# The opening of a two-layer diffusion backbone: token loads first, weights of the conditioning held in the array, first projection products fed one feature tile at a time

## The chip, the cores and the metric

One core of a Trainium2 chip runs the kernel. The metric is device time in microseconds, the median of several runs of the program.

## The reference

The reference is a two-layer backbone over 512 latent tokens and 256 context tokens of width 1024. Each layer starts from a conditioning vector `c` (latents) or `c_ctx` (context). What matters here is the beginning of layer 0:

```
s_c, s_cc = silu(c), silu(c_ctx)
sh1, sc1, g1, sh2, sc2, g2 = split(s_c @ w_ada[0] + b_ada[0], 6)     # w_ada[0]: 1024 x 6144; the same with s_cc for the context
h  = rms_norm(x,   norm_mix[0]) * (1 + sc1)  + sh1
hc = rms_norm(ctx, norm_mix[0]) * (1 + csc1) + csh1
p, pc = h @ w_in[0], hc @ w_in[0]                                    # w_in[0]: 1024 x 6144
```

After it come three mixers (retention, grouped attention, pooling), a gated merge, an output projection and a feed-forward part (dense in layer 0, eight experts of which each token takes two in layer 1). All of it is in 32-bit floats.

## The kernel before

Features stand on the 128 partitions, so a feature dimension of 1024 is eight tiles `k` (KT = 8), and the tokens (T0 = 768: 512 latent, 256 context) lie along the free dimension. A product in full precision is made of three fast passes: a value is split into a high part and a low part, and TensorE (PE) computes high x high, low x high and high x low (lines 330 to 332, in `proj`). The class `Stream` (from line 40) holds all weights in their order of use. Its `pump` loads 1 MB pieces into `raw` tiles (two buffers) through the queue of SP, and splits halves into `wh` (ScalarE, ACT, line 94) and `wl` (VectorE, DVE, line 95). `take(n)` hands out n halves.

Each engine runs its instructions in one order. Outside the experts of layer 1 a planner of the framework writes that order: it takes the instructions by their place in the program, but lets a later one go ahead where its own cost estimates say that the earlier one is not ready. It also places all waits. Tiles come from pools with a fixed count of buffers, and a new tile waits until the old user of its buffer has finished.

The opening (lines 985 to 1113) works as follows.

- **Loads.** The queue of SP issues the six token tiles `xtok` (128 tokens each, 512 KB, line 1013) between four pieces of `w_ada` (`araw`, 1 MB, line 1017, three buffers). ACT's queue issues the small vectors (`crow`, `vrow`, `rdb`).
- **`turn(t)`** takes the squares of a token tile on ACT (line 1045), transposes its eight feature tiles on PE (line 1050) and copies them from PSUM to `xT`, half on ACT and half on DVE.
- **Conditioning.** `scol` holds silu of `c` and `c_ctx` as columns. Only column groups j = 0 to 3 of `w_ada` (512 columns each: shift and scale of the first norm) are needed here. For j = 0, 1 and 3 `ada_direct` makes the two columns of `scol` the standing operand and streams 512 columns of `w_ada` past them, eight times, summed in PSUM (line 279). The result is two rows, which ACT copies (line 281) and PE turns into columns (line 284). A 32-bit product of this kind appears in the trace as two passes, so that a group is 16 passes. For j = 2 DVE multiplies and adds (lines 158 and 160, 16 operations), GpSimd (POOL) cuts the sums into three parts, and PE adds over the partitions with 24 tiny products (line 234).
- **Norm.** `rr`, 1 / rms of each token, is spread over the partitions by PE (line 1082); DVE multiplies `xT` with it (line 1086) into `u`, which lies in the memory of `xtok`. `modulation` turns shift and scale into `AB` (lines 269 and 270). `norm0(k)` makes the high part `hh` on ACT (line 1101) and the low part `hl` on DVE (lines 1105 and 1106); for k = 3 and 7 ACT does the work of line 1105. Groups j = 0 and 2 give `AB` for k = 0 to 3, groups j = 1 and 3 for k = 4 to 7.
- **Products.** `mix_phase(0)` then runs the units of the mixers, `u0` and `u1` first, each for 512 latent and 256 context tokens.

Of the kernel before, what the change touches and what calls it, by code (L numbers as in the profile page):

```python
# [35 lines left out]
# vec-tile rows (rows of 128 values, turned into columns on the chip)  # L36
# [76 lines left out]
def tile_backbone(  # L113
# [19 lines left out]
    # ---------------------------------------------------------------- weights, in order of use  # L133
# [11 lines left out]
    def ada_sum(li, j, nv):  # L145
        """512 columns of w_ada, multiplied and summed over k ahead of the sum over partitions."""
# [28 lines left out]
    # column tiles of w_in: name -> tile index  # L175
# [7 lines left out]
    # ---------------------------------------------------------------- constants  # L183
# [14 lines left out]
    def rsqrt(out_ap, v, n, make=None):  # L198
        """out = v ** -0.5 for a small [128, n] tile, or a wide one with tiles from make."""
# [36 lines left out]
    # ---------------------------------------------------------------- plan of the layers  # L236
# [5 lines left out]
    st = {}          # state handed from one part to the next  # L242
    later = []       # steps to be placed between the groups of products that follow
# [10 lines left out]
    # ================================================================ small vectors, modulation  # L254
# [3 lines left out]
    AB = vp.tile([128, 2, 2, KT], F32, name="AB")      # stream (latent/context), A or B, k  # L258
# [5 lines left out]
    def modulation(li, which, norm_row, k0=0, k1=KT):  # L264
        """A = gain * (1 + scale), B = shift of the norm in front of a mixer, for both streams."""
# [6 lines left out]
    def ada_direct(j, raws, mid=None):  # L272
        """The same columns for layer 0, all of the sum on the tensor engine."""
        p = st["mm"].tile([128, 512], F32, name="mm")
        for k in range(KT):
            w = raws[k // 4].rearrange("p (k m) -> p k m", k=4)[:, k % 4]
            if k == 4 and mid:
                mid()
            PE.matmul(p[:2], scol.rearrange("p (s k) -> p k s", s=2)[:, k], w, start=(k == 0), stop=(k == KT - 1))
        r = st["sp"].tile([2, 512], F32, name="adarow")  # L280
        A.activation(r, p[:2], AF.Copy)
        p2 = st["mm"].tile([128, 512], F32, name="mm")
        for q in range(4):
            PE.transpose(p2[:, 2 * q:2 * q + 2], r[:, 128 * q:128 * q + 128], ident[:2, :2])
        ada_store(0, j, 2, p2[:, :8].rearrange("p (q s) -> p s q", s=2))
# [21 lines left out]
    # ================================================================ mixers  # L307
    class Mixer:
# [6 lines left out]
        def proj(self, name, both):  # L315
            """One column tile of w_in for all tokens (both) or for those that are queries."""
# [19 lines left out]
            return fn  # L336

# [60 lines left out]
        def stat(self, name, parts):  # L398
            """(mean square + eps) ** -0.5 of a head's queries or keys, [128, tiles]."""
# [24 lines left out]
        def spread(self, r, n):  # L424
            """[128, n] per token -> the same value on all partitions, [128, n * 128] in PSUM."""
# [11 lines left out]
        # ---- retention  # L437
        def retention(self):
            li, T, mt = self.li, self.T, st["mt"]
            for pr in range(2):  # L440
                yield from self.wait(f"rq{pr}", f"rk{pr}")
                # of each head: its queries' high part twice, its keys' high part and low part
# [19 lines left out]
                for h in (2 * pr, 2 * pr + 1):  # L462
# [4 lines left out]
                    # values by token, centred over the head's width: the group norm's mean  # L467
# [11 lines left out]
                    # decays as a function of query - key  # L479
# [80 lines left out]
        # ---- attention  # L560
# [88 lines left out]
        # ---- pooling  # L649
# [133 lines left out]
    def square_in(mt, c0, c1):  # L783
        """Adds the square of one feature tile of x to the running sum."""
# [63 lines left out]
    # ================================================================ dense feed-forward  # L848
# [67 lines left out]
    # ---------------------------------------------------------------- order of all the weights  # L916
# [8 lines left out]
    def plan_layer(li):  # L925
        m = mixers[li]
        for nm in order[li].split():
            if nm.startswith("ada"):
# [35 lines left out]
    def run(ph, gen=None):  # L964
        """The units of a phase; gen is advanced by a step in front of each and at its ticks."""
# [12 lines left out]
    # ================================================================ start: inputs, modulation, first norm  # L978
# [24 lines left out]
    with tc.tile_pool(name="start", bufs=1, reuse_waits="tile") as sp, tc.tile_pool(name="start_ps", bufs=8, space=PSUM, reuse_waits="tile") as mm:  # L1003
        st["mm"], st["sp"] = mm, sp
        st["accr"] = lambda t: (lambda r: [r[:, :512], r[:, 512:]])(sp.tile([128, D], F32, name="junk"))
        xtok = sp.tile([128, 6, D], F32, name="xtok")
        crow = sp.tile([16, 128], F32, name="crow")
# [7 lines left out]
        def load_ada(j, h):  # L1015
            r = rawp.tile([128, 2048], F32, name="raw") if (j, h) == (3, 0) else sp.tile([128, 2048], F32, name="araw", bufs=3)
            SY.dma_start(r.rearrange("p (k m) -> p k m", k=4), ada_src(0, j, h))
# [13 lines left out]
        # conditioning vectors as columns: silu  # L1031
        p = mm.tile([128, 512], F32, name="mm")
# [6 lines left out]
        # x with the features first, 1 / rms of each token  # L1039
        ss = sp.tile([128, 6], F32, name="ss")  # L1040
        xT = sp.tile([128, KT, T0], F32, name="xT0")

        def turn(t):
            junk = sp.tile([128, D], F32, name="junk")
            A.activation(junk, xtok[:, t], AF.Square, accum_out=ss[:, t:t + 1])
            for h in range(2):
                p = mm.tile([128, 512], F32, name="mm")
# [4 lines left out]
                if h:  # L1052
                    V.tensor_copy(dst, pv)
                else:
                    A.activation(dst, pv, AF.Copy)

        turn(0)
        p = mm.tile([128, 512], F32, name="mm")
        for li in range(2):
            PE.transpose(p[:, 128 * li:128 * li + R_N], vrow[:, li], ident[:R_N, :R_N])  # L1060
            V.tensor_copy(vec[li], p[:, 128 * li:128 * li + R_N])
            V.tensor_scalar(gnh[li], vec[li][:, R_GN:R_GN + 4], 0.5, None, op0=OP.mult)
        ada_direct(0, [raws[0, h] for h in range(2)])
        use = ada_sum(0, 2, 2)
        use(0)(raws[2, 0])
        for t in range(1, 6):
# [5 lines left out]
        acc2 = use(1)(raws[2, 1])  # L1072
        for a in ((1, 0), (1, 1), (3, 0), (3, 1)):
            load_ada(*a)
        rb = []
        u = xtok.rearrange("p a b -> p (a b)").rearrange("p (k t) -> p k t", k=KT)

        def spread_rr():
            for t0, t1 in ((0, 4), (4, 6)):
                p = mm.tile([128, 512], F32, name="mm")  # L1080
                for t in range(t0, t1):
                    PE.transpose(p[:, 128 * (t - t0):128 * (t - t0) + 128], rr[:, t:t + 1].to_broadcast([128, 128]), ident)
                rb.append(p[:, :128 * (t1 - t0)])
            for k in range(KT):
                for s, (c0, c1) in enumerate(((0, L), (L, T0))):
# [695 lines left out]
```

## Time and profile before

| | us |
|---|---|
| median of 3 runs | 3347.98 |
| lowest and highest run | 3347.87, 3348.95 |
| profiled execution, first to last instruction (span) | 3350.0 |
| PE busy in the span | 3229.9 |
| DVE busy | 2190.0 |
| ACT busy | 1449.6 |
| first product of `w_in` starts at | 55.98 |

The profiled execution is one execution of its own; its time is listed as its span alone, which is 2.0 us above the median of the runs. PE is the engine with the most work. Times in the trace count from the first instruction. The granted clock of PE has two levels, 0.5 (1.2 GHz) and 1.0 (2.4 GHz). The profile holds no record of it for the first 15.7 us and prints 1.00 there.

### The profile page before, as it was taken

Reading aid. Unit: us, or ns where it says so; the run is one execution under the profiler, and the core shown is the slowest. Engines: PE = TensorE matmul, PEld = TensorE weight load, DVE = VectorE, ACT = ScalarE, POOL = GpSimd, SP = SyncE. Lnnn points to the kernel's source line nnn. Section 1 sums busy time; section 2 is a strip of 40 time slices with the busy share of each in tenths; the row PEclk is TensorE's granted clock in tenths of the full one; section 3 lists DMA queues with packets and bytes.
Section 4 is the critical chain, followed back from the end, with each engine's and each line's share of the span. In section 5 each row is a group of like instructions: output and inputs, shape, how many; then the busy total and the mean of one; then the engine's idle time right before and its main releaser. Section 6 shows DMA issues by size and latency. Waiting matters only on the chain. (4 is left out here: it accounts for less than half of the span.)

```text
span 3350.0 us, 43794 instructions
## 1 busy us (share of the span) xinstructions
PE 3229.9 (96%) x17203; PEld 2680.2 (80%) x17204; DVE 2190.0 (65%) x3319; ACT 1449.6 (43%) x2001; POOL 277.4 (8%) x250
## 2 busy tenths in 40 slices
PE   7999999999999999999999997999999999999995
PEld 4887788888888888888778886777777777777774
DVE  6478777467454444456766566865798855885586
ACT  4334343224122111134434434754576645664564
POOL 1011221101010000000011011010000000000001
PEclk9999999999999999999999998999999999999998
DMA  7133342542232332323222447976699965996595
GB/s 267 65 109 122 107 139 92 183 151 73 79 126 98 104 113 89 101 89 124 91 85 88 132 158 255 358 252 226 229 386 359 315 244 195 321 336 238 197 326 205
DMA packets 298312, 605.00 MB, mean 181 GB/s; under 512 B 12410, under 2 KB 100636, under 8 KB 297564
## 3 DMA queue, kind: packets, MB, share of 16 engines
q1 hardware_dynamic: 285232, 555.26, 46.8%
q0 software_dynamic: 10720, 44.83, 4.1%
q8 instruction: 152, 2.49, 0.3%
q10 hardware_dynamic: 2124, 1.74, 0.2%
q14 instruction: 84, 0.69, 0.1%
HBM read 561.15 MB, written 40.63 MB: 180 GB/s over the span
## 5 line engine op out<-in xcount | busy, mean ns | idle before, releaser
L95 DVE TENSOR_TENSOR wl<-raw,wh 128x1024 fp32r<-128x1024 f32 x889 | 1052.3, 1233 | 208.9 <-ACT wh L94 195.4
L94 ACT ACTIVATE wh<-raw 128x1024 fp32r<-128x1024 f32 x892 | 884.1, 1053 | 501.5 <-PE mm L887 152.6
L331 PE MATMUL mm<-hl,wh 128*128 128x512 f32 (+1 forms) x1232 | 436.3, 354 | 6.1 <-DVE hl L846 6.1
L330 PE MATMUL mm<-hh,wh 128*128 128x512 f32 (+1 forms) x1232 | 440.5, 358 | 0.3 <-DVE mod L288 0.3
L332 PE MATMUL mm<-hh,wl 128*128 128x512 f32 (+1 forms) x1232 | 435.1, 353 | 0.0
L864 PE MATMUL mm<-hh,wh 128*128 128x512 f32 (+1 forms) x896 | 302.8, 339 | 1.0 <-ACT hh L841 1.0
L865 PE MATMUL mm<-hl,wh 128*128 128x512 f32 (+1 forms) x896 | 301.9, 337 | 1.6 <-DVE hl L846 1.0
L866 PE MATMUL mm<-hh,wl 128*128 128x512 f32 (+1 forms) x896 | 301.4, 337 | 0.0
L331 PEld LDWEIGHTS mm<-hl,wh 128*128 128x128 f32 x1232 | 235.7, 191 | 36.3 <-DVE hl L846 7.5
L330 PEld LDWEIGHTS mm<-hh,wh 128*128 128x128 f32 x1232 | 235.6, 191 | 34.6 <-issue 3.9
L332 PEld LDWEIGHTS mm<-hh,wl 128*128 128x128 f32 x1232 | 235.4, 191 | 30.3 <-issue 0.2
L865 PEld LDWEIGHTS mm<-hl,wh 128*128 128x128 f32 x896 | 170.2, 190 | 21.0 <-DVE hl L846 2.0
L1375 PE MATMUL y<-wh,gth 128*128 128x512 f32 x448 | 180.0, 402 | 6.5 <-PEq L1529 1.1
L864 PEld LDWEIGHTS mm<-hh,wh 128*128 128x128 f32 x896 | 169.9, 190 | 19.7 <-ACT hh L841 1.5
L866 PEld LDWEIGHTS mm<-hh,wl 128*128 128x128 f32 x896 | 170.1, 190 | 17.6
L1361 PE MATMUL b<-wl,xh 128*128 128x512 f32 x448 | 178.1, 398 | 4.1 <-DVE wl L95 4.1
L1359 PE MATMUL b<-wh,xh 128*128 128x512 f32 x448 | 180.9, 404 | 0.0
L1359 PE MATMUL a<-wh,xh 128*128 128x512 f32 x448 | 178.8, 399 | 1.8 <-DVEq L1529 1.0
L1376 PE MATMUL y<-wh,gtl 128*128 128x512 f32 x448 | 177.3, 396 | 0.8 <-DVE gtl L222 0.8
L160 DVE SCALAR_TENSOR_TENSOR acc<-raw,scol,acc 128x512 f32<-128x512 f32 x224 | 166.2, 768 | 18.0 <-DMA raw<-in_w_ada_dram 16.6
L1360 PE MATMUL a<-wh,xl 128*128 128x512 f32 x448 | 177.5, 396 | 0.0
L1377 PE MATMUL y<-wl,gth 128*128 128x512 f32 x448 | 177.2, 396 | 0.0
(414 smaller groups left out, 6077.5 us busy)
## 6 DMA issues: line engine op xcount, KB each, us to landing
raw<-in_moe_w_dram SPq DMA_DIRECT2D x336, 1024.0 KB, 7.6
raw<-in_w_in_dram SPq DMA_DIRECT2D x48, 1024.0 KB, 5.3
raw<-in_ffn_w_dram SPq DMA_DIRECT2D x42, 1024.0 KB, 4.9
raw<-in_w_ada_dram SPq DMA_DIRECT2D x41, 1024.0 KB, 5.3
raw<-in_w_branch_dram SPq DMA_DIRECT2D x12, 1024.0 KB, 6.2
gsp<-gst POOLq DMA_DIRECT2D x24, 384.0 KB, 2.9
gt<-gsp SPq DMA_DIRECT2D x24, 384.0 KB, 3.5
raw<-in_w_out_dram SPq DMA_DIRECT2D x8, 1024.0 KB, 5.7
```

What stands on the lines that cost most here:

```text
L94: nc.scalar.activation(hv, r, AF.Copy)
L95: (nc.gpsimd if self.n_split in self.on_pool else nc.vector).tensor_sub(lv, r, hv)
L330: PE.matmul(pv, wh[:, k], st["hh"][:, k, c0:c1], start=(k == 0), stop=False)
L331: PE.matmul(pv, wh[:, k], st["hl"][:, k, c0:c1], start=False, stop=False)
L332: PE.matmul(pv, wl[:, k], st["hh"][:, k, c0:c1], start=False, stop=(k == KT - 1))
L864: PE.matmul(pv, wh[:, k], st["hh"][:, k, c0:c1], start=(k == 0), stop=False)
L865: PE.matmul(pv, wh[:, k], st["hl"][:, k, c0:c1], start=False, stop=False)
L866: PE.matmul(pv, wl[:, k], st["hh"][:, k, c0:c1], start=False, stop=(k == KT - 1))
L1359: PE.matmul(p, xh[:, k], wh, start=(k == 0), stop=False)
L1360: PE.matmul(p, xl[:, k], wh, start=False, stop=False)
L1361: PE.matmul(p, xh[:, k], wl, start=False, stop=(k == KT - 1))
L1375: PE.matmul(y[:, n], gh[:, j], wh[:, 0, s], start=first and j == 0, stop=False)
```

## The change

The token tiles are all loaded first, then four pieces of `w_ada` (now 256 columns by all 1024 rows, four buffers), then two pieces of `w_in` with their splits. The parts of `turn` are as before; ACT copies one PSUM bank in four and DVE the rest. `ada_direct(j)` is turned round: the 128 x 128 blocks of `w_ada` stand in the array and the two columns of `scol` stream past them, so that the results are columns at once. All four groups go that way, each in two halves; each half is 2 x 8 products of two columns. Groups 0 and 2 stand before the norm, and the halves of groups 1 and 3 between its steps. After each `norm0(k)` a new function `first(k)` runs the products of that feature tile for `u0` (512 and 256 tokens) and `u1` (512 tokens), held in three PSUM banks across all eight k. `proj_open`, the first unit of the mixer phase, copies them out and computes the context tokens of `u1`. The PSUM pool of the products (three banks) is opened ahead of the opening, whose own pool shrinks from eight banks to five.

```diff
+        def ada_direct(j):
+        p = st["sps"].tile([128, 512], F32, name="sps")
+        def half(h, raw):
+            w = raw.rearrange("p (k m) -> p k m", k=KT)
+            for q in range(2):
+                for k in range(KT):
+                    PE.matmul(p[:, 4 * h + 2 * q:4 * h + 2 * q + 2], w[:, k, 128 * q:128 * q + 128],
+                              scol.rearrange("p (s k) -> p k s", s=2)[:, k], start=(k == 0), stop=(k == KT - 1))
+            if h:
+                ada_store(0, j, 2, p[:, :8].rearrange("p (q s) -> p s q", s=2))
+        return half
...
+        def proj_open(self):
+            done, (wh, wl) = st["open"]
+            for i, (c0, c1, p) in enumerate(done):
+                self.evac("u0" if i < 2 else "u1", c0, c1, p, c0 == 0, c1 == T0)
+            p = st["mm"].tile([128, 512], F32, name="mm")
...
-        for t, a in ((0, (0, 0)), (1, (0, 1)), (2, (2, 0)), (3, None), (4, None), (5, (2, 1))):
+        for t in range(6):
             load_x(t)
-            if a:
-                load_ada(*a)
+        for a in ((0, 0), (0, 1), (2, 0), (2, 1)):
+            load_ada(*a)
+        ws.raw_bufs = 1
+        ws.pump()
...
+        sum0, rb = ada_direct(0), []
+        sum0(0, raws[0, 0])
...
+        sum0(1, raws[0, 1])
+        for a in ((1, 0), (1, 1)):
             load_ada(*a)
+        sum2 = ada_direct(2)
+        sum2(0, raws[2, 0])
+        sum2(1, raws[2, 1])
+        for a in ((3, 0), (3, 1)):
+            load_ada(*a)
         modulation(0, 0, R_NMIX, 0, 4)
...
+        w0, w1 = ws.take(2)
+        open_ = [(w, c0, c1, st["mm0"].tile([128, 512], F32, name="mm")) for w, c0, c1 in ((w0, 0, L), (w0, L, T0), (w1, 0, L))]
+        def first(k):
+            for (wh, wl), c0, c1, p in open_:
+                pv = p[:, :c1 - c0]
+                PE.matmul(pv, wh[:, k], st["hh"][:, k, c0:c1], start=(k == 0), stop=False)
+                PE.matmul(pv, wh[:, k], st["hl"][:, k, c0:c1], start=False, stop=False)
+                PE.matmul(pv, wl[:, k], st["hh"][:, k, c0:c1], start=False, stop=(k == KT - 1))
+        sum1, sum3 = ada_direct(1), ada_direct(3)
+        steps = [lambda: sum1(0, raws[1, 0]), lambda: sum1(1, raws[1, 1]), lambda: sum3(0, raws[3, 0]), lambda: sum3(1, raws[3, 1])]
         for k in range(4):
             norm0(k)
-        ada_direct(3, [raws[3, h] for h in range(2)])
+            first(k)
+            steps[k]()
         modulation(0, 0, R_NMIX, 4, 8)
+        ws.raw_bufs = 2
+        ws.pump()
+        SY.dma_start(st["xsp"], xT)
+        SY.dma_start(rope_t, tab[:, :2048].rearrange("p (a b) -> p a b", a=4))
...
         for k in range(4, 8):
             norm0(k)
+            first(k)
```

## Rows read from the trace of the kernel before

**Rows 1.** The page: busy time of PE, granted clock in 40 slices.

```profile
PE 3229.9 (96%) x17203; PEld 2680.2 (80%) x17204; DVE 2190.0 (65%) x3319; ACT 1449.6 (43%) x2001; POOL 277.4 (8%) x250
...
PEclk9999999999999999999999998999999999999998
```

**Rows 2.** Windows from the first product on: busy us by engine, clock, DMA.

```profile
55.90:60.19 4.29, 4.29 (x15) 3.36 (x13) 3.41 (x9) 3.37 (x6) 0.00 (x0) 0.60 1.10 383
...
64.53:67.67 3.14, 3.14 (x18) 2.71 (x17) 1.73 (x3) 2.01 (x5) 1.47 (x2) 1.00 0.11 27
```

**Rows 3.** Groups of PE by form, 55.9 to 67.66: two of six.

```profile
L330 PE MATMUL mm<-hh,wh 128*128 128x512 f32 x10 | 4.8, 476 | 0.0
...
L330 PE MATMUL mm<-hh,wh 128*128 128x256 f32 x8 | 2.2, 281 | 0.0
```

**Rows 4.** Timeline of the opening: start us, length us.

```profile
5.54 1.97 PE L1050 MATMUL mm<-ident,xtok 128*128 128x128 f32 x8
...
8.92 1.06 ACT L1045 ACTIVATE junk<-xtok 128x1024 f32<-128x1024 f32 x1
...
37.65 1.00 DVE L217 SCALAR_TENSOR_TENSOR rr<-rs_a,rs_r 128x6 f32<-128x6 f32 x1
...
47.31 0.23 DVE L269 SCALAR_TENSOR_TENSOR AB<-mod,vec 128x4 f32<-128x4 f32 x2
...
55.98 0.50 PE L330 MATMUL mm<-hh,wh 128*128 128x512 f32 x1
```

**Rows 5.** Waits in the queue of SP, 0 to 60 us.

```profile
SPq L1013 <- DMA vrow<-in_norm_mix_dram: 5.8, 1, 5.8
```

**Rows 6.** Windows, 10 to 20 us: DMA share, GB/s last.

```profile
10.00:20.00 10.00, 9.40 (x17) 1.47 (x17) 2.07 (x12) 3.02 (x8) 0.00 (x0) 1.00 1.00 379
```

**Rows 7.** Groups by form, 0 to 64: busy us, mean ns.

```profile
L279 PE MATMUL mm<-araw,scol 128*2 128x512 f32 x40 | 22.0, 701 | 2.0 <-DVE scol L1037 2.0
...
L1106 DVE TENSOR_TENSOR hl<-xtok,hh 128x768 fp32r<-128x768 f32 x7 | 6.6, 955 | 0.1
L1101 ACT ACTIVATE hh<-xtok,AB 128x512 fp32r<-128x512 f32 x8 | 6.4, 801 | 1.2 <-DVE AB L269 1.2
...
L1105 DVE TENSOR_SCALAR xtok<-xtok,AB 128x512 f32<-128x512 f32 x6 | 3.3, 542 | 0.8 <-ACT hh L1101 0.8
```

**Rows 8.** Timeline of PE at the router of layer 1.

```profile
2006.37 1.07 PE L1182 MATMUL s<-ident,xl 128*128 128x128 f32 x8
2007.27 1.85 PE L1186 MATMUL po<-rw,xl 128*128 128x8 f32 x16
2008.98 0.46 PE L759 MATMUL mm<-hh,wh 128*128 128x256 f32 x1
2009.24 0.41 PE L760 MATMUL mm<-hl,wh 128*128 128x256 f32 x1
2009.45 0.41 PE L761 MATMUL mm<-hh,wl 128*128 128x256 f32 x1
```

**Rows 9.** Windows of the same place.

```profile
2007.27:2008.98 1.71, 1.71 (x19) 1.71 (x17) 0.36 (x2) 1.51 (x3) 0.00 (x0) 1.00 0.00 0
...
2009.10:2012.50 3.40, 3.40 (x18) 3.40 (x18) 1.41 (x6) 1.43 (x2) 0.00 (x0) 0.50 0.58 230
```

**Rows 10.** Windows of PE during the transposes of the opening.

```profile
25.95:29.36 3.41, 3.41 (x18) 0.50 1.04 386
29.36:31.20 1.84, 1.84 (x18) 1.00 1.05 388
```

**Rows 11.** Timeline of PE and its weight loads, 56 to 61.

```profile
56.86 0.33 PEld L331 LDWEIGHTS mm<-hl,wh 128*128 128x128 f32 x1
57.29 0.63 PE L331 MATMUL mm<-hl,wh 128*128 128x512 f32 x1
...
57.71 0.63 PE L332 MATMUL mm<-hh,wl 128*128 128x512 f32 x1
...
60.19 0.19 PEld L330 LDWEIGHTS mm<-hh,wh 128*128 128x128 f32 x1
```

More of the change, by code (lines that the diff above doesn't have):

```diff
@@ L270, in modulation @@
             V.tensor_copy(AB[:, s, 1, k0:k1], sh)
[L272 to L285, printed above, removed]
+    def ada_direct(j):
[9 more added lines that the diff above has]
+        return half
     def ada_store(li, j, nv, p):
@@ L336, in proj @@
             return fn
+        def proj_open(self):
+            done, (wh, wl) = st["open"]
+            for i, (c0, c1, p) in enumerate(done):
+                self.evac("u0" if i < 2 else "u1", c0, c1, p, c0 == 0, c1 == T0)
+            ready.add((0, "u0"))
+            p = st["mm"].tile([128, 512], F32, name="mm")
+            pv = p[:, :C]
+            for k in range(KT):
+                PE.matmul(pv, wh[:, k], st["hh"][:, k, L:], start=(k == 0), stop=False)
+                PE.matmul(pv, wh[:, k], st["hl"][:, k, L:], start=False, stop=False)
+                PE.matmul(pv, wl[:, k], st["hh"][:, k, L:], start=False, stop=(k == KT - 1))
+            self.evac("u1", L, T0, pv, False, True)
+            ready.add((0, "u1"))
         def evac(self, name, c0, c1, p, first, last):
@@ L927, in plan_layer @@
         for nm in order[li].split():
+            if li == 0 and nm == "u0":
+                add_cols(w_in[0], 128 * WT[nm])
+                unit("mix0", 0, lambda hs: m.proj_open())
+                continue
             if nm.startswith("ada"):
@@ L1001, in tile_backbone @@
     ws.stage(wpool, 3, limits["mix0"])
-    with tc.tile_pool(name="start", bufs=1, reuse_waits="tile") as sp, tc.tile_pool(name="start_ps", bufs=8, space=PSUM, reuse_waits="tile") as mm:
-        st["mm"], st["sp"] = mm, sp
-        st["accr"] = lambda t: (lambda r: [r[:, :512], r[:, 512:]])(sp.tile([128, D], F32, name="junk"))
+    mm0 = ExitStack()
+    st["mm0"] = mm0.enter_context(tc.tile_pool(name="mix_mm0", bufs=3, space=PSUM, reuse_waits="tile"))
+    with tc.tile_pool(name="start", bufs=1, reuse_waits="tile") as sp, tc.tile_pool(name="start_ps", bufs=5, space=PSUM, reuse_waits="tile") as sps:
+        st["sps"] = sps
         xtok = sp.tile([128, 6, D], F32, name="xtok")
-        crow = sp.tile([16, 128], F32, name="crow")
+        crow = st["adap"].tile([128, 2, 512], F32, name="acc")[:16, 0, :128]
         A.dma_start(crow[0:8], c.rearrange("o (k p) -> (o k) p", p=128))
@@ L1029, in tile_backbone @@
         A.dma_start(rdb, bass.AP(tensor=ret_decay.tensor, offset=ret_decay.offset, ap=[[0, 128], [1, 16]]))
-        p = mm.tile([128, 512], F32, name="mm")
+        p = sps.tile([128, 512], F32, name="sps")
         PE.transpose(p[:, :16], crow, ident[:16, :16])
@@ L1051, in turn @@
                 dst = xT[:, 4 * h:4 * h + 4, 128 * t:128 * t + 128]
-                if h:
+                if t % 2 and h:
+                    A.activation(dst, pv, AF.Copy)
+                else:
                     V.tensor_copy(dst, pv)
[L1054 to L1066, printed above, removed]
+        for t in range(6):
             turn(t)
@@ L1071, in tile_backbone @@
         rsqrt(rr, vv, 6)
-        acc2 = use(1)(raws[2, 1])
-        for a in ((1, 0), (1, 1), (3, 0), (3, 1)):
-            load_ada(*a)
[L1075 to L1085, printed above, removed]
-                    V.tensor_mul(u[:, k, c0:c1], xT[:, k, c0:c1], rb[s])
@@ L1088, in tile_backbone @@
-        ada_direct(1, [raws[1, h] for h in range(2)], spread_rr)
-        ada_sum_unit(0, 2, 2)([None, acc2])
-        modulation(0, 0, R_NMIX, 0, 4)
-        ws.pump()
-        SY.dma_start(st["xsp"], xT)
-        SY.dma_start(rope_t, tab[:, :2048].rearrange("p (a b) -> p a b", a=4))
-        A.dma_start(ptab, tab[:, 2048:2112].rearrange("p (a b c) -> p a b c", a=4, b=2))
-        A.dma_start(g2b, bass.AP(tensor=b_ada.tensor, offset=b_ada[1, 5 * D:6 * D].offset, ap=[[0, 128], [1, D]]))
-        A.activation(lg2, rdb, AF.Exp)
@@ L1097, in tile_backbone @@
-        V.tensor_scalar(lgc, lg2, -1.0, None, op0=OP.mult)
+        p = sps.tile([128, 512], F32, name="sps")
+        for li in range(2):
+            PE.transpose(p[:, 128 * li:128 * li + R_N], vrow[:, li], ident[:R_N, :R_N])
+            V.tensor_copy(vec[li], p[:, 128 * li:128 * li + R_N])
+            V.tensor_scalar(gnh[li], vec[li][:, R_GN:R_GN + 4], 0.5, None, op0=OP.mult)
+        sum0, rb = ada_direct(0), []
+        sum0(0, raws[0, 0])
+        for t0, t1 in ((0, 4), (4, 6)):
+            p = sps.tile([128, 512], F32, name="sps")
+            for t in range(t0, t1):
+                PE.transpose(p[:, 128 * (t - t0):128 * (t - t0) + 128], rr[:, t:t + 1].to_broadcast([128, 128]), ident)
+            rb.append(p[:, :128 * (t1 - t0)])
@@ L1637, in mix_phase @@
         T = m.T
-        with tc.tile_pool(name="mix_mm", bufs=3, space=PSUM, reuse_waits="tile") as mm, tc.tile_pool(name="mix_s2", bufs=2, space=PSUM) as s2, \
+        mm0 = st["mm0"] if li == 0 else st["mm0x"].enter_context(tc.tile_pool(name="mix_mm", bufs=3, space=PSUM, reuse_waits="tile"))
+        with tc.tile_pool(name="mix_s2", bufs=2, space=PSUM) as s2, \
                 tc.tile_pool(name="mix_po", bufs=1, space=PSUM, reuse_waits="tile") as po:
-            st["mm"], st["s2"], st["po"] = mm, s2, po
+            st["mm"], st["s2"], st["po"] = mm0, s2, po
             n3, n2 = (15, 8) if li == 0 else (8, 14)
@@ L1722, in tile_backbone @@
     ad0.close()
+    st["mm0x"] = mm1 = ExitStack()
     mix_phase(1)
+    mm1.close()
     dump("x3l", st["xl"])
```

18 lines of the change are left out of this document (14 added, 4 removed).

## Prediction

> **What bounds the kernel now.** I read the page first, then windows over the start, then the timeline of the opening, and then looked elsewhere in the trace for an operation like the one that the change brings in. PE is busy 96% of the span, and the clock was granted nearly throughout [rows 1]. The profiled execution took 3350.0 us by its span, 2.0 more than the median of the runs; I work out a difference against its trace and add it to the median. A difference of 0.2% (6.7 us) is about what a measurement of this kernel can tell from none.
>
> The opening is the exception. The first product of `w_in` starts at 55.98 us, and the clock had just fallen, so that the 11 products of 512 columns begun before 60.19 (15 PE instructions touch that window, three of them turns of a result row, one at its edge) mostly took 0.43 us each [rows 2, 4, 11]. From 60.19 to 67.66, 30 - 11 = 19 products of 512 columns and 24 of 256 fill 7.47 us, which gives 0.24 and 0.12 us at the upper level [rows 3]; PE has no gap there [rows 2]. At 0.24 the 11 first ones are worth 2.6 us, so the old kernel does as well as one whose PE runs nothing but mixer work at full speed from 60.2 - 2.6 = 57.5 us. Behind that point PE is the bound, so the change is worth what it does to this one number. I call it the equivalent start.
>
> **What is removed.** Groups 0, 1 and 3 of the conditioning cost 48 passes (40 of them 22.0 us busy, part of it at the lower level) [rows 7]. With them go the copies and turns of the result rows, and for group 2 DVE's sums, which held `rr` back to 38.65 us [rows 4]. None of this is left on the path.
>
> **Loads.** Six token tiles and one piece of `w_ada` are 4.2 MB. At the 379 GB/s of 10 to 20 us [rows 6] that is 11 us; with some 2 us before data flows, everything for the first sum has landed at about 13 us. In the old kernel the second token load stood in SP's queue 5.8 us for the landing of a small vector [rows 5]; I assume that four or five loads ahead cover such a wait, and price it under the rivals. The 48 transposes of the tokens begin at about 5.5 us, when the first tile lands [rows 4], and need 0.21 us each at the lower level (16 starts in 3.41 us, the two cut by the edges left out) [rows 10], together 10.2 us. So the first narrow pass can start between 13 us (loads) and about 19 us (if ACT's copies, behind its squares, hold the PSUM banks). I take 15. The two `w_in` loads and three splits put ahead of groups 1 and 3 are off the path: these groups wait in PE's queue far longer than for their data. The `xsp`, table and vector loads move behind the second modulation; none is read before the mixers.
>
> **The new sums.** This is the largest term. A 32-bit product appears as two passes, so a half of a group is 2 x 8 x 2 = 32 passes, each with a 128 x 128 weight load for two columns, and all four groups are 256 passes. The router holds the same form: 128 x 128 standing, eight columns streaming, 16 passes in 1.71 us, 0.107 us each at the upper level [rows 8, 9]. The load sets this pace, not the columns. At the upper level all sums are 27.4 us. The old sums of three groups were 48 passes at about 0.43, 20.6 us. So even at full clock PE has more conditioning work than before.
>
> At the lower level I find no such pass. Below, it is 0.107 (the load does not slow). Above, it is 0.213: products of 256 columns with the same size of load start 0.21 us apart there [rows 8], so a load fits into that. Weight loads grow from 0.19 to 0.33 us in the trace when the clock is halved [rows 11], so I take 0.213, and 54.6 us for all sums.
>
> Which level will it be? At the router PE did 16 passes, eight transposes and 16 passes from 2004.66 to 2008.98 without idle time, at the upper level, and at 2009.1 the clock fell to half although PE was busy throughout [rows 8, 9]. Transposes alone do not do this: after 3.4 us of them back to back the clock rose [rows 10]. So long runs of narrow passes lose the clock. I take three quarters of the narrow passes and of the products between them at the lower level; bounds are all and half.
>
> The Trainium skill (TensorE: Matmul & The Clock Gate, section "Why this matters for your kernels") advises to keep TensorE continuously busy to get and hold the full clock. By that rule the sums would run at the upper level, which is the first rival below. The router's rows disagree with it for narrow passes.
>
> **The path after the change.**
> - Groups 0 and 2, 128 passes, three quarters slow: 0.75 x 27.3 + 0.25 x 13.7 = 23.9 us. Eight transposes (spreading `rr`, turning vectors) add 1.7. `AB` is ready at 15 + 25.6 = 40.6 us, where it was 47.3 [rows 4].
> - Groups 1 and 3, 23.9 us again, and `first(0)` to `first(3)`. One is six products of 512 columns and three of 256: 1.8 us at the upper level, 3.2 at the lower. Four are 7.2 or 12.8, at three quarters 11.4. PE ends them at 75.9.
> - Then PE waits for the second modulation and `norm0(4)`: store and `AB` about 0.4, `hh` 0.8 and about 0.6, `hl` 0.96 [rows 7], 3 us with hand-overs. 78.9.
> - `first(4)` at the lower level 3.2; the next three at 1.8, by PE as well as by DVE (0.54 + 0.4 + 0.96, less where ACT takes a part) [rows 7]. 87.5.
> - All three product banks are then full. The mixer's buffers lie in the memory of the opening, so the copies out start only behind the last `norm0`. I take 1 us, between nothing and 2. 88.5.
> - Of this, eight `first` worth 14.4 us at the upper level are mixer work done. The equivalent start is 74.1 us, 16.6 later than before.
>
> In short, after `AB` the old kernel needed 10.2 us to its equivalent start. The new one must still put 13.7 to 27.3 us of sums and 4 us of waits there, and `AB` comes only some 7 us sooner. Forecast: 3348.0 + 16.6 = about 3365 us. With everything slow `AB` is at 44.0, and the start at 82.3 (+24.8, 3373), or 3377 if the first pass starts at 19. With half slow it is 65.5 (+8, 3356).
>
> **Rivals.**
> - *The upper level holds through the narrow passes.* Then `rr` limits: six squares of 1.06 us with 0.19 for the sum, three copies, and 13 small DVE operations from about 9 us [rows 4] make it ready at 20.5. With group 0's first half before it and the rest behind, `AB` is at 31.6; sums and four `first` end at 52.5, the last four with waits at 63.7; the equivalent start is 49.3, a gain of 8.2: about 3340. The tight weight-load pace speaks for it, the fall at 2009.1 [rows 9] against. Between +24.8 and -8.2 the sign turns where about three quarters of the narrow passes run at the upper level.
> - *The lower level does not slow a narrow pass.* Then groups 0 and 2 end at 32.4, groups 1 and 3 with slow products at 58.9, and the equivalent start is 57.1: no change, 3348. For it: nothing in the trace has such a pass at the lower level. Against: the loads of 0.33 us [rows 11]. The Trainium skill (same page, section "LDWEIGHTS (loading the stationary operand)") gives a load as its columns over 1.2, 107 ns, with no word of the clock's level. The pace at the upper level agrees with it, no row shows the lower, and the sum by it would be this rival's.
> - *The loads are not ahead after all.* If the wait of 5.8 us in SP's queue [rows 5] comes back ahead of the later token tiles, all moves by that: 3371.
> - *The planner's order for the rest comes out differently.* PE idles 120 us in the span, so some 10 us more or less are possible, and no row tells which. I count this at 3340, where it would hide the forecast.
>
> **Chances.** Forecast 0.64, its own range 3356 to 3377; upper level holds 0.15; slow clock without slow passes 0.11; late loads 0.05; another order 0.05. Slower: 0.64 + 0.05, and 0.01 of the third case, 0.70. Within 0.2%: 0.10 of the third and 0.03 of the second, 0.13. Faster: 0.12 + 0.05 = 0.17. The range from 3340 to 3377 holds the forecast's own range and the third case, and leaves out about half of the second, some of the fifth and the tails.
>
> **What would show it.** The windows from 15 to 80 us should show PE busy with the clock near 0.5 for most of it. Narrow passes should start 0.21 us apart there and 0.107 where the clock is up; `AB` at 38 to 46 us; the last `first` ending at 80 to 97 us; and the work behind shifted by one constant. The prediction is wrong if the clock stays at 1.0 through the sums, if a half's 32 passes take 3.4 us at the lower level, or if PE runs the products while the sums' data are still landing.

## The result and the profile after

The changed kernel takes 3379.20 us (median of 4 runs, 3376.08 to 3382.21), the kernel before 3348.47 on the same chip (4 runs, 3347.87 to 3349.76). The ratio is 1.0086, with a 95% interval of 1.0074 to 1.0098. It is slower, as forecast, but by about 31 us and not by 17: the median lies 2.2 us above the upper end of the predicted range. The profiled execution took 3377.84 us, with a span of 3376.0.

The page, with busy times and the granted clock in 40 slices, to be read against [rows 1]:

```profile
PE 3256.6 (96%) x17375; PEld 2724.1 (81%) x17376; DVE 2181.2 (65%) x3306; ACT 1445.8 (43%) x1995; POOL 279.4 (8%) x246
...
PEclk6999999999999999999999998999999999999998
```

PE is busy 26.7 us longer than before, and the span is 26.0 us longer. The clock row differs from before in its first slice alone (the first 84 us): the loss is in the opening and is never earned back. Windows over that stretch, with busy us of the engines, then clock, DMA share and GB/s:

```profile
20.00:34.00 14.00, 13.63 (x65) 13.54 (x64) 1.51 (x12) 1.76 (x2) 0.00 (x0) 0.50 1.09 349
34.00:49.50 15.50, 14.96 (x70) 14.90 (x70) 7.85 (x20) 0.25 (x1) 0.00 (x0) 0.50 0.55 179
49.50:67.00 17.50, 14.13 (x51) 12.45 (x52) 9.71 (x16) 7.99 (x12) 0.00 (x0) 0.50 0.38 121
67.00:84.40 17.40, 17.38 (x114) 16.51 (x113) 1.45 (x4) 0.00 (x0) 0.00 (x0) 0.79 0.63 231
84.40:96.50 12.10, 9.55 (x36) 7.39 (x36) 7.01 (x14) 7.64 (x13) 2.18 (x3) 0.73 0.32 125
```

From 20 to 67 us the clock stands at its lower level, although PE is busy for 42.7 of these 47 us. The Trainium skill (TensorE: Matmul & The Clock Gate, section "Why this matters for your kernels") advises to keep TensorE continuously busy for the full clock. From 20 to 34 us PE had 13.63 of 14.00 us busy and did not get it, so the trace does not bear the advice out for these passes. The clock was already down when the first of them started, at 19.73 us: it fell while PE stood idle.

```profile
17.00:19.73 2.73, 0.00 (x0) 0.03 (x1) 1.37 (x9) 1.33 (x3) 0.00 (x0) 0.90 1.09 349
75.22:78.71 3.49, 3.49 (x34) 3.49 (x32) 0.00 (x0) 0.00 (x0) 0.00 (x0) 1.00 1.07 357
```

The timeline of the same stretch (start, length, engine, line; in brackets the idle time ahead and who ended it). Line 281 is a narrow pass, 1128 to 1130 are the products of `first`, 371 copies a product bank out, 347 is `proj_open`:

```profile
19.73 6.96 PE L281 MATMUL sps<-scol,araw 128*128 128x2 f32 x32 [2.79 <-DMA araw<-in_w_ada_dram]
...
26.71 6.91 PE L281 MATMUL sps<-scol,araw 128*128 128x2 f32 x32
...
35.82 13.65 PE L281 MATMUL sps<-scol,araw 128*128 128x2 f32 x64
...
49.71 0.23 DVE L269 SCALAR_TENSOR_TENSOR AB<-mod,vec 128x4 f32<-128x4 f32 x2
...
50.78 1.50 PE L1128 MATMUL mm<-hh,wh 128*128 128x512 f32 x3 [1.30 <-ACT hh L1114]
...
54.38 0.79 PE L1129 MATMUL mm<-hl,wh 128*128 128x512 f32 x1 [2.09 <-DVE hl L1119]
...
56.67 6.82 PE L281 MATMUL sps<-scol,araw 128*128 128x2 f32 x32
...
67.06 3.80 PE L281 MATMUL sps<-scol,araw 128*128 128x2 f32 x32
...
75.22 3.63 PE L281 MATMUL sps<-scol,araw 128*128 128x2 f32 x32
...
79.02 5.36 PE L281 MATMUL sps<-scol,araw 128*128 128x2 f32 x32
...
84.62 0.23 DVE L269 SCALAR_TENSOR_TENSOR AB<-mod,vec 128x4 f32<-128x4 f32 x2
...
95.92 1.34 ACT L371 ACTIVATE ubuf<-mm 128x512 f32<-128x512 f32 x3
...
96.55 0.39 PE L347 MATMUL mm<-hh,wh 128*128 128x256 f32 x1 [0.82 <-ACT ubuf L371]
```

The first `AB` comes at 49.71 us, 2.4 us later than the old one [rows 4]. The second comes at 84.62. In the trace of before it stands at 56.62, so it is 28.0 us later:

```profile
56.62 0.24 DVE L269 SCALAR_TENSOR_TENSOR AB<-mod,vec 128x4 f32<-128x4 f32 x2
```

At the lower level 32 passes take 6.82 us, 0.213 each. At 75.22 us, where the clock is up (the window 75.22 to 78.71 above), they take 3.63 us, 0.113 each. `proj_open` starts at 96.55 us. With 14.4 us of mixer work done by then the equivalent start is 82.15 us, where it was 57.5: 24.65 us later.

The waits in the queue of SP, 0 to 80 us (line waiting, for what, sum, count, longest), to be read against [rows 5]:

```profile
SPq L1033 <- DMA xtok<-in_x_dram: 4.2, 2, 2.8
SPq L1037 <- DMA rdb<-in_ret_decay_dram: 4.2, 1, 4.2
```

SP still stands for landings, 8.4 us in these two rows: once ahead of `w_ada` (line 1037), for `rdb`, a small vector that ACT's queue had issued, and twice ahead of token tiles (line 1033).

### The profile page after: what moved, and what is told of

It is laid out like the page before. It is cut to its first block, busy times and chain, and to the rows that moved or that the text cites. A ratio compares the mean times of both kernels' runs of the same rounds, so it can differ in the third digit from the quotient of the medians.

```text
span 3376.0 us, 44115 instructions
## 1 busy us (share of the span) xinstructions
PE 3256.6 (96%) x17375; PEld 2724.1 (81%) x17376; DVE 2181.2 (65%) x3306; ACT 1445.8 (43%) x1995; POOL 279.4 (8%) x246
## 5 line engine op out<-in xcount | busy, mean ns | idle before, releaser
L331 PE MATMUL mm<-hl,wh 128*128 128x512 f32 (+1 forms) x1200 | 425.5, 355 | 5.4 <-DVE hl L861 5.4
L330 PE MATMUL mm<-hh,wh 128*128 128x512 f32 (+1 forms) x1200 | 429.4, 358 | 0.3 <-DVE mod L288 0.3
L332 PE MATMUL mm<-hh,wl 128*128 128x512 f32 (+1 forms) x1200 | 424.3, 354 | 0.0
L879 PE MATMUL mm<-hh,wh 128*128 128x512 f32 (+1 forms) x896 | 302.3, 338 | 1.1 <-ACT hh L856 1.1
L880 PE MATMUL mm<-hl,wh 128*128 128x512 f32 (+1 forms) x896 | 301.6, 337 | 1.8 <-DVE hl L861 1.2
L881 PE MATMUL mm<-hh,wl 128*128 128x512 f32 (+1 forms) x896 | 301.0, 336 | 0.0
L1398 PE MATMUL a<-wl,xh 128*128 128x512 f32 x448 | 177.3, 396 | 0.0
```

The lines of the kernel that those rows point to most:

```text
L330: PE.matmul(pv, wh[:, k], st["hh"][:, k, c0:c1], start=(k == 0), stop=False)
L331: PE.matmul(pv, wh[:, k], st["hl"][:, k, c0:c1], start=False, stop=False)
L332: PE.matmul(pv, wl[:, k], st["hh"][:, k, c0:c1], start=False, stop=(k == KT - 1))
L879: PE.matmul(pv, wh[:, k], st["hh"][:, k, c0:c1], start=(k == 0), stop=False)
L880: PE.matmul(pv, wh[:, k], st["hl"][:, k, c0:c1], start=False, stop=False)
L881: PE.matmul(pv, wl[:, k], st["hh"][:, k, c0:c1], start=False, stop=(k == KT - 1))
```

## The experiments

Three groups of runs, each on one chip, each compared with the kernel before on that chip. In the expectations A is the theory that I held at the time, B its rival. In the first group A says that the two-column form of the sums costs the time, because the clock is lost and each pass then takes twice as long; B puts it down to the rest of the rebuild, late loads and the new order.

### The same sums, 128 columns wide

Each standing block meets 64 copies of the pair of columns. The result is read from the first copy; the loads, the order and all else are those of the changed kernel.

```diff
-                PE.matmul(p[:, 4*h+2*q:4*h+2*q+2], w[:, k, 128*q:128*q+128], scol...[:, k], ...)
+                PE.matmul(p[:, 256*h+128*q:256*h+128*q+128], w[:, k, 128*q:128*q+128],
+                          scol...[:, k][:, None, :].to_broadcast([128, 64, 2]), ...)
```

> The changed kernel, with 128 columns (the two of scol, 64 times over) in place of 2 streaming past each standing block; one column pair of each 64 is used. Theory A (the narrow passes cost what they do because they let the clock fall): the wide passes keep the clock up, a pass takes 0.11 to 0.13 us where a narrow one took 0.213, AB for k 0 to 3 comes at 36 to 41 us in place of 49.7, and the time is 3347 to 3358 us, 20 us or more below the changed kernel. Theory B (the clock falls whatever the number of columns, or a pass of 128 columns adds its columns to its load): a pass takes 0.21 us or more, and the time is 3375 us or more.

Measured: 3350.56 us, before 3350.07; ratio 1.0000 (0.9991 to 1.0010). The timeline of this kernel:

```profile
19.72 1.81 PE L281 MATMUL sps<-scol,araw 128*128 128x128 f32 x10 [1.97 <-DMA araw<-in_w_ada_dram]
...
21.45 3.83 PE L281 MATMUL sps<-scol,araw 128*128 128x128 f32 x22
...
25.77 10.89 PE L281 MATMUL sps<-scol,araw 128*128 128x128 f32 x96
...
36.89 0.24 DVE L269 SCALAR_TENSOR_TENSOR AB<-mod,vec 128x4 f32<-128x4 f32 x2
...
60.82 0.24 DVE L269 SCALAR_TENSOR_TENSOR AB<-mod,vec 128x4 f32<-128x4 f32 x2
```

Its windows, with the clock third from the end:

```profile
20.00:24.00 4.00, 4.00 (x24) 4.00 (x23) 1.51 (x10) 0.00 (x0) 0.00 (x0) 0.57 1.09 348
24.00:34.00 10.00, 10.00 (x92) 10.00 (x91) 8.25 (x17) 2.00 (x2) 0.00 (x0) 1.00 1.09 348
34.00:49.50 15.50, 13.49 (x104) 12.56 (x104) 10.44 (x20) 8.11 (x13) 0.00 (x0) 1.00 1.09 349
```

Nothing in the program differs but the columns that stream, 64 times as many. The first pass starts at the same time as in the changed kernel, and here too the clock is down at first (0.57 in 20 to 24 us). But under the wide passes it is back by 24 us and stays up, where under the narrow ones it stayed down to 67 us. From then on 96 passes take 10.89 us, 0.113 each. That is also what a narrow pass takes at the upper level, so a wide pass is not cheaper in itself: what it changes is the level. The first `AB` comes 12.8 us earlier than in the changed kernel, the second 23.8 us earlier, and the whole loss is gone. This is A, and it leaves the rest of the rebuild with no measurable effect in sum.

### Rows instead of columns

The changed kernel with its sums in the old orientation: two columns stand, 256 columns of `w_ada` stream, for all four groups.

```diff
-            for q in range(2): for k in range(KT): PE.matmul(p[:, ...2 columns], w[:, k, 128*q:128*q+128], scol...[:, k], ...)
+            for k in range(KT): PE.matmul(p[:2, 256*h:256*h+256], scol...[:, k], w[:, k], ...)
+            (with h = 1: copy of the row by ACT, four turns by PE)
```

> The changed kernel with its new loads and its products fed one feature tile at a time, but all four conditioning groups with scol standing and w_ada streaming, as the old kernel had it for three of them (256 columns a pass, 32 passes a group). Theory A (the standing weights are the loss, by their load pace at the lower level): a group takes about 6.9 us once the clock is up, AB for k 0 to 3 comes at 38 to 43 us, and the time is 3346 to 3357 us. Theory B (the loss comes from the late loads and from having four groups on the tensor engine, not from the orientation): 3365 us or more.

Measured: 3354.69 us; ratio 1.0011 (1.0001 to 1.0020). The row of 32 passes in its timeline, and a window:

```profile
30.75 7.07 PE L280 MATMUL sps<-araw,scol 128*2 128x256 f32 x32
```

```profile
30.00:40.00 10.00, 8.91 (x46) 3.79 (x47) 8.88 (x18) 5.63 (x7) 0.00 (x0) 1.00 1.09 348
```

These passes take 0.221 us each with the clock up, for twice the columns of a wide pass above, and a group has 32 of them in place of 64. The second `AB` comes at 63.13 us. So the slow part is not tied to the new loads and the new order: another form of the sums between the same loads and products brings back some 25 of the 29 us.

### The small vectors behind the first loads

Four small loads go from ACT's queue to SP's, behind the first pieces of `w_ada` and `w_in`.

```diff
-            A.dma_start(vrow[r0:r0 + n], ...)
+            SY.dma_start(vrow[r0:r0 + n], ...)
 (the same for rdb, ptab, g2b)
```

> The changed kernel with the small vectors (vrow, rdb, ptab, g2b) issued from SP's queue behind the first loads of w_ada and w_in, so that no load of w_ada waits for one of them. Theory A (late data moved the first narrow pass from the forecast 15 to 19.7 us, and all behind it): the first narrow pass at 12.5 to 15 us, AB 4 to 7 us sooner, 3372 to 3376 us. Theory B (the loads are covered): first pass sooner or not, the time stays at 3379 us.

Measured: 3379.65 us; ratio 1.0088 (1.0071 to 1.0104). A miss as an experiment: it was to bring the sums forward and it held them back. In its timeline PE waits for a small vector ahead of the first narrow pass:

```profile
30.34 0.36 PE L1087 MATMUL sps<-ident,vrow 74*128 74x74 f32 x1 [14.81 <-DMA vrow<-in_attn_kn_dram]
...
30.49 6.91 PE L281 MATMUL sps<-scol,araw 128*128 128x2 f32 x32
```

The first pass is 10.8 us later than in the changed kernel and `proj_open`, at 103.93 us, 7.4 us later, yet the span is 3375.4, 0.6 less than 3376.0. The two traces show where the 7.4 us go. PE is still 7.4 us late at 222 us, 2.3 at 367 and 0.3 at 449. In between, the changed kernel loses time that this run does not: PE waits 2.1 us for a tile of a mixer (`sl`, line 541), and the clock falls for a while, to 0.94 in the mean of 300 to 330 us and 0.96 in 330 to 370, where it is 1.00 here. PE's window from 300 us, of the changed kernel and then of this run (busy us, clock, DMA share, GB/s):

```profile
300.00:330.00 30.00, 27.88 (x126) 0.94 0.29 97
```

```profile
300.00:330.00 30.00, 29.87 (x143) 1.00 0.44 142
```

From 420 to 450 us PE idles 6.8 us in the changed kernel and 4.3 here, which takes up the rest. Why this run meets neither that wait nor those falls is not shown.

### Standing weights alone, in the kernel before

The kernel before, with groups 0, 1 and 3 as standing blocks and two columns; loads, DVE's group 2 and the norm stay.

```diff
-            PE.matmul(p[:2], scol...[:, k], w, ...)            # 512 columns of w_ada stream
+        for q in range(4): for k in range(KT):
+            PE.matmul(p[:, 2*q:2*q+2], w[:, 128*q:128*q+128], scol...[:, k], ...)
```

> The kernel before with one thing changed: groups 0, 1 and 3 of the conditioning with the weights standing (64 narrow passes each), loads, group 2 and all else as they were. Theory A (narrow passes at the lower level are the loss): groups take 13.7 us each, the first product of w_in starts 8 to 12 us later than 55.98, the time is 3354 to 3362 us. Theory B (the loss lies in the new arrangement of loads and products): 3347 to 3351 us.

Measured: 3378.28 us; ratio 1.0079 (1.0062 to 1.0096). The direction was A's, the size far more than I expected. A row of its timeline, and a window:

```profile
47.28 12.09 PE L280 MATMUL mm<-scol,araw 128*128 128x2 f32 x56
```

```profile
37.40:76.66 39.26, 27.91 (x150) 27.46 (x150) 17.80 (x51) 3.01 (x5) 4.48 (x4) 0.50 0.40 130
```

These passes take 0.216 us each, the clock is at its lower level, and the first product of `w_in` starts at 76.66 us instead of 55.98, 20.7 us later. The profiled span is 27.7 us longer than that of before; where the other 7 us arise behind the opening is not shown. By the medians this one part of the change, put alone into the old kernel, costs as much as the whole change.

### The same, 128 columns wide

This run belongs to the second group. It widens the passes of the run above, to see whether its 28 us were the clock or the form itself.

```diff
-            PE.matmul(p[:, 2*q:2*q+2], w[:, 128*q:128*q+128], scol...[:, k], ...)
+            PE.matmul(p[:, 128*q:128*q+128], w[:, 128*q:128*q+128], scol...[:, k][:, None, :].to_broadcast([128, 64, 2]), ...)
```

> The kernel before with groups 0, 1 and 3 standing, with 128 columns streaming past each block in place of 2. Theory A (the 28 us of the narrow form in this place are the clock): 3347 to 3353 us. Theory B (they come from standing weights as such, whose blocks need all eight feature tiles of a group at once and so wait longer for the loads): 3360 us or more.

Measured: 3350.99 us, before 3351.99; ratio 0.9998 (0.9988 to 1.0007). A pass and a window near the end of its opening:

```profile
40.39 3.74 PE L280 MATMUL mm<-scol,araw 128*128 128x128 f32 x32
```

```profile
37.40:51.70 14.30, 14.30 (x142) 14.29 (x141) 12.95 (x30) 4.42 (x7) 3.10 (x3) 0.95 0.98 368
```

The clock is up, a pass takes 0.117 us, and the first product starts at 51.72 us. This is A. The two pairs, narrow and wide, in the old and in the new arrangement, give the same answer.

### The small vectors on POOL's queue

The changed kernel with the four small loads on the queue of POOL: does the late first pass come from SP's waits?

```diff
-            A.dma_start(vrow[r0:r0 + n], ...)
+            G.dma_start(vrow[r0:r0 + n], ...)
 (the same for rdb, ptab, g2b)
```

> The changed kernel with the small vectors (vrow, rdb, ptab, g2b) issued from POOL's queue, whose completions SP's loads do not wait for. They land early this time, unlike in the run before, where they stood behind 6 MB. Theory A (the late first load of w_ada moved the whole chain of sums, which is bound by the tensor engine from there on): the first narrow pass at 13 to 16 us in place of 19.7, AB at 43 to 46, 3373 to 3376 us. Theory B (the work behind the opening takes up a few us of delay, as when the first pass came at 30.5 us and the time did not change): 3378 to 3381 us.

Measured: 3375.67 us, before 3351.99; ratio 1.0074 (1.0058 to 1.0089). From its timeline:

```profile
17.77 4.09 PE L281 MATMUL sps<-scol,araw 128*128 128x2 f32 x32 [0.72 <-DVE vv L1082]
...
44.89 0.24 DVE L269 SCALAR_TENSOR_TENSOR AB<-mod,vec 128x4 f32<-128x4 f32 x2
```

SP's wait for `rdb` is gone, and the first pass starts at 17.77 us, 2.0 earlier and now behind DVE's work, not behind a load. It does not reach the 13 to 16 us that I expected. `AB` is 4.8 us earlier, 2.0 of it by this start and 2.9 because the first 32 passes took 4.09 us and not 6.96: here PE had idled only 0.72 us, and the passes found the clock up. They lost it within the run: the next 32, at 21.88 us, took 6.92. So narrow passes lost the upper level here and did not win it back in the changed kernel (0.50 from 20 to 67 us). The span is 6.7 us shorter, and the time lies in A's range. But in the medians this is not told apart from the changed kernel: 1.0074 and 1.0086 have overlapping intervals.

### Wide, and POOL's queue

Both edits together.

```diff
+                PE.matmul(..., scol...[:, k][:, None, :].to_broadcast([128, 64, 2]), ...)
+            G.dma_start(vrow[r0:r0 + n], ...)   # and rdb, ptab, g2b
```

> The wide passes of the first experiment together with the small vectors on POOL's queue. Theory A (with the clock up, the chain of loads and sums sets the end): first pass at 13 to 16 us, AB at 31 to 34, 3343 to 3347 us, faster than both kernels. Theory B (delays of the opening up to about 5 us are taken up behind it): 3348 to 3352 us.

Measured: 3349.06 us, before 3351.99; ratio 0.9995 (0.9986 to 1.0004). The time lies in B's range; A's marks are missed too, with the first pass at 18.11 us and the first `AB` at 34.72. The second `AB` comes at 58.69 us, 2.1 earlier than with the wide sums alone. So at the upper level, too, the late loads are worth some two microseconds in the trace of the opening; in the time the two wide runs are not told apart (0.9995 and 1.0000, with overlapping intervals).

### Wide, without the fed products

The wide sums, but `u0` and `u1` are ordinary units of the mixers, as before; `first` and `proj_open` are left out.

```diff
-            first(k)
...
-                unit("mix0", 0, lambda hs: m.proj_open())
```

> The wide passes without the products fed one feature tile at a time: u0 and u1 are ordinary units of the mixer phase again, behind all the sums in the program. Theory A (the fed products stand between the sums that the second half of the norm waits for): sums end at about 52 us, the second AB at 53 in place of 60.8, the products of the first four feature tiles fill the wait for the norm, 3345 to 3348 us. Theory B (the feeding hides the norm and is the useful part of the change): 3353 us or more.

Measured: 3347.64 us, before 3351.99; ratio 0.9986 (0.9977 to 0.9996). From its timeline:

```profile
38.30 14.51 PE L281 MATMUL sps<-scol,araw 128*128 128x128 f32 x128
...
53.05 0.24 DVE L269 SCALAR_TENSOR_TENSOR AB<-mod,vec 128x4 f32<-128x4 f32 x2
```

The sums of groups 1 and 3 now run in one piece, and the second `AB` comes 16.2 us behind the first, where the fed form needs 23.9. This is A. So the feeding delays the second half of the norm. In the time it costs some 4.7 us (0.0014 between the two ratios), though the intervals of the two overlap at their ends.

### Narrow, without the fed products

The same edit, with the two-column sums of the changed kernel, in the third group of runs. Does dropping the feeding also help where the clock is low?

```diff
-            first(k)
...
-                unit("mix0", 0, lambda hs: m.proj_open())
```

> The changed kernel with its narrow passes, but without the products fed one feature tile at a time: u0 and u1 are ordinary units of the mixer phase behind all the sums. Theory A (the narrow sums at the lower level set the time; the fed products only stand between them, and run at the lower level for it): the first AB stays at 49.7 us, the second comes at 77 to 79 in place of 84.6, the products start at the lower level and reach the upper after 3 to 4 us, 2 to 5 us less than the changed kernel, 3374 to 3377 us. Theory B (feeding hides the norm): 3382 us or more.

Measured: 3381.29 us, before 3351.84; ratio 1.0094 (1.0079 to 1.0109). There is no gain, and the time falls between the two theories' ranges. The timeline shows why:

```profile
48.60 0.23 DVE L269 SCALAR_TENSOR_TENSOR AB<-mod,vec 128x4 f32<-128x4 f32 x2
...
54.72 6.82 PE L281 MATMUL sps<-scol,araw 128*128 128x2 f32 x32
...
65.66 3.89 PE L281 MATMUL sps<-scol,araw 128*128 128x2 f32 x32
...
83.54 0.23 DVE L269 SCALAR_TENSOR_TENSOR AB<-mod,vec 128x4 f32<-128x4 f32 x2
```

Between the two `AB` lie 34.9 us, as in the changed kernel. Without `first` the planner puts products of ordinary units between the same halves of the sums, so the order that the edit was to remove came back. The edit does not test what I meant it to test.

### Wide, without the fed products, POOL's queue

The three edits together.

```diff
+                PE.matmul(..., scol...[:, k][:, None, :].to_broadcast([128, 64, 2]), ...)
-            first(k)
+            G.dma_start(vrow[r0:r0 + n], ...)   # and rdb, ptab, g2b
```

> Wide passes, no fed products, small vectors on POOL's queue. Theory A (the three terms add up: clock, order of sums and products, start of the first sum): the second AB at 50 to 51.5 us, 1 to 3 us less than with the wide passes and no fed products alone, a ratio to the kernel before of 0.9975 to 0.9985. Theory B (the start of the first sum is taken up by later waits once the sums are short): the ratio stays at 0.9986 or above.

Measured: 3346.28 us (11 runs), before 3351.84 (15 runs); ratio 0.9983 (0.9974 to 0.9992). From its timeline:

```profile
17.32 1.35 PE L281 MATMUL sps<-scol,araw 128*128 128x128 f32 x10 [0.71 <-DVE vv L1078]
...
34.45 0.23 DVE L269 SCALAR_TENSOR_TENSOR AB<-mod,vec 128x4 f32<-128x4 f32 x2
...
36.30 0.49 PE L330 MATMUL mm<-hh,wh 128*128 128x512 f32 x1 [3.67 <-ACT hh L1110]
...
36.63 16.13 PE L281 MATMUL sps<-scol,araw 128*128 128x128 f32 x128
...
53.00 0.23 DVE L269 SCALAR_TENSOR_TENSOR AB<-mod,vec 128x4 f32<-128x4 f32 x2
```

`AB` is at 34.45 us, 12.9 earlier than in the old kernel, and the time is less than that of both kernels. The gain of 0.17% is small, but its interval excludes no change. The ratio lies in A's range, but A's mechanism is not borne out: the second `AB` comes at 53.00 us, not at 50 to 51.5, and the run without POOL's queue had it at 53.05. The 2.4 us by which the first `AB` is earlier are used up behind it. PE waits 3.67 us for `hh`, where it had been 1.30, and then the clock is down for a while (0.58 in 37.5 to 41 us), so that the 128 passes take 16.13 us in place of 14.51. The ratios 0.9983 and 0.9986 are not told apart, so what POOL's queue adds to the gain is not shown.

## Why the prediction was right in direction and short in size

The mechanism was the right one; several sizes were off. By the prediction's own steps, the equivalent start was to be 74.1 us and was 82.15, 8.05 later:

- **First narrow pass: 15 us forecast, 19.73 measured, +4.7.** The step that failed says that "four or five loads ahead cover such a wait" in SP's queue. They did not: SP stood 4.2 us for tokens and 4.2 us for `rdb`, and PE waited 2.79 us for `w_ada` directly ahead of the first pass. The value was just beyond the upper bound of 19. Removing the wait brought the pass to 17.77 only, where DVE's work was next, so about 2 of the 4.7 us were the loads. The rest is the work ahead of the first pass, which I had put too early within my range.
- **Groups 0 and 2: 25.6 us from the first pass to `AB` forecast, 30.0 measured, +4.4.** The assumed share of three quarters was the second step that failed: all 128 passes ran at the lower level. With POOL's queue, where the first pass found the clock up, this stretch took 27.1 us. By these two traces some 2.9 of the 4.4 us come from the clock having fallen while PE waited for `w_ada`, a price of the late load that the prediction did not have.
- **From the first `AB` to the second: 35.7 us forecast (75.9 + 0.4 - 40.6), 34.9 measured, -0.8.** Two errors cancel, by luck. The sums of groups 1 and 3 took 6.82 + 3.80 + 3.63 + 5.36 = 19.6 us, not 23.9, because the clock rose between 67 and 84 us. In turn PE waited 1.1 us behind `AB` for `hh` and 2.1 us for `hl`. I had counted that wait only behind the second modulation, not behind the first.
- **From the second `AB` to the equivalent start, with its 14.4 us: 12.2 forecast (88.5 - 76.3), 11.9 measured.** The waits for norm and banks held: 0.82 us for the banks where I took 1.

The sum over all 256 passes came out close, but by luck: all of the first 128 ran at the lower level, and less than half of the others. The group of line 281, busy us and mean ns:

```profile
L281 PE MATMUL sps<-scol,araw 128*128 128x2 f32 x256 | 47.1, 320 | 2.8 <-DMA araw<-in_w_ada_dram 2.8
```

Three quarters at the lower level gave 0.75 x 54.6 + 0.25 x 27.4 = 47.8 us. The bound of 0.213 us for a pass at the lower level, taken from products with a load of the same size [rows 8], was exact. One reading of the prediction is off, though no term hangs on it: the transposes of [rows 10] began at 24.23 us, so the clock rose after 5.1 us of them, not 3.4.

With 24.65 in place of 16.6 the prediction's sum gives 3372.7 us, still inside its range. What carried the median beyond it is the third step that failed, to add a difference of traces to the median of before as if the profiled execution stood for that median. The profiled executions differ by 26.0 us, so another 1.3 us arose behind the opening, and the medians by 30.7. The rest, 4.7 us, lies between the executions. The prediction put before's profiled execution 2.0 us above the median, but this sets a span against a time: with the 1.84 us that the run of after has outside its span, before's profiled execution is 3351.8, 3.4 above its median of 3348.47, and after's 3377.84 is 1.4 below its own. The last 0.5 us is the median of before, 3348.47 here and 3348.0 in the sum. On the chips of the experiments the median of before was 3350.07 to 3351.99, so part of this is the spread of runs, and the prediction's bound of 3377 left no room for it.

**The rivals.** That the upper level holds was refuted by the clock, and the run with wide sums shows what it would have looked like: no loss, though also not the 8.2 us of gain. That a low clock does not slow a pass was refuted by 6.82 us for 32. The Trainium skill (TensorE: Matmul & The Clock Gate, section "LDWEIGHTS (loading the stationary operand)") gives a load as its columns over 1.2, 107 ns for 128, with no word of the clock's level. A pass of 0.113 us at the upper level fits that, 0.213 at the lower does not. Late loads did occur, as a smaller addition to the forecast. Another order did not hide the loss: the shift is 24.65 us at the end of the opening and 26.0 at the end of the kernel.

**Shown and not shown.** Shown, by two pairs of kernels, is that the narrow form of the sums alone costs the whole loss, and that it comes with the low clock. Not shown is what exactly about the columns lets the clock fall. Times of single executions behind the opening also differ by a few us, by waits and falls of the clock that come in one run and not in another, as with the vectors behind the first loads; what decides them is open. The spread of the changed kernel's runs (6.1 us in 4 runs) has no shown cause.

## What to carry to other kernels

Price a product with few streaming columns by its weight load, and look in the trace whether a run of them keeps the clock: at the lower level a pass took 0.213 us here and at the upper 0.113, and the products of 512 columns between the sums 0.43 and 0.23. Where such products cannot be avoided, widen what streams, even with copies of the same columns: 128 in place of two saved 29 us here. Ahead of a norm that waits for several sums, let them run in one piece: products fed between them put the second half of it 7.8 us later here, with the clock up.

## What the hardware showed that was not expected

- Work added made the kernel faster: 64 times as many columns in the same 256 passes took the ratio to the kernel before from 1.0086 to 1.0000, and the busy time of line 281 from 47.1 to 31.7 us.
- The clock can be low for 47 us in a row while PE is busy for 42.7 of them; every kernel here with two-column sums lost it, and with wide ones it was down in the opening only for stretches of a few us.
- The fall is not certain for a short run of such passes. At the router, where the kernel before fell to the lower level just behind 32 passes of eight columns [rows 9], the changed kernel did the same passes and stayed up. Its timeline there, and a window:

```profile
2031.40 1.85 PE L1223 MATMUL po<-rw,xl 128*128 128x8 f32 x16
...
2034.02 1.85 PE L1223 MATMUL po<-rw,xl 128*128 128x8 f32 x16
```

```profile
2035.72:2038.00 2.28, 2.28 (x21) 2.28 (x21) 1.54 (x6) 1.55 (x2) 0.00 (x0) 1.00 0.41 165
```

- A load on SP's queue can stand for the landing of a small vector that another queue issued: 5.8 us before [rows 5], 4.2 after, none once the vectors went through POOL's queue.
